# Output projection: which engine makes four combinations of y, and where its weight slots lie

## The chip, the core and the metric

One core of a Trainium2 chip runs the whole kernel. The core has a matrix engine (TensorE; PE in the profile, its weight loads PEld), a vector engine (VectorE, DVE), an activation engine (ScalarE, ACT), a general engine (GpSimd, POOL) and a queue that issues the transfers (SyncE, SP). Each engine takes its own instructions strictly in the order in which they stand in its queue, and waits on semaphores for the others. The metric is the device time of one execution in microseconds.

## What is computed

The reference is one layer of a hybrid decoder for 512 tokens (T) of width 2048 (D): a windowed attention branch and a gated DeltaNet branch, merged by gates, and one last projection that is added to the residual stream:

```python
y_a = a_out @ w_o_swa
y_b = o.reshape(B, T, DN_VAL).astype(x.dtype) @ w_o_dn
y = jax.nn.sigmoid(mg_a) * y_a + jax.nn.sigmoid(mg_b) * y_b
return x + gate * (y @ w_out)
```

The change concerns the last two lines. All matrix products are made to nearly full float32 accuracy: each operand is split into a high part (a rounding cast, on ScalarE) and a low part (operand minus high part, on VectorE), and three matmuls, high by high, high by low and low by high, add up in PSUM. This split is the helper at L52 and L53, and the three matmuls are L223 to L225; so work of many places in the program shows under these lines.

## The kernel before

The kernel runs through a start, the DeltaNet, its output projection, the attention, and the method `finish`, in which the change lies. `finish` has two stages.

**The stage ahead** makes y. It goes through 16 tiles j of 128 channels by 512 tokens. For each, `channel_tile` multiplies the attention's output, which lies in the tiles hh and hl (16 x 512 elements per partition each), by 2048 rows of a weight (raw, loaded from in_w_os, 1 MB). The product (PSUM tile mm) gets gated and merged with the other branch (m and yb, each loaded from DRAM; L1226 and L1227), and y's tile is stored to DRAM (y_d, L1228). Its first 256 tokens are split at once into a11 (j below 8) or a12 (j from 8 on), and for j below 8 the sum of its two token halves is split into s3.

**The output stage** multiplies y by w_out (2048 x 2048) by a scheme of seven products in place of eight, for two halves n of the columns. With y cut into four blocks (channels below and above 1024, tokens below and above 256; `lo` and `hi` are the token halves), the left operands are a11, a12, a22, and four combinations s1 = a21 - a22, s2 = -(s1) - a11, s3 = a11 + a21, s4 = a21 - a22 + a11 - a12. The right operands are sums of quarters of w_out that lie in slots a, b and c of two 1 MB tiles each (raw for slot a, rawb and rawc for the others):

```python
order = [
    ("m1", "a11", "a", []),
    ("m7", "s3", "b", [add("a", "b"), add("b", "c")]),
    ("m5", "s1", "a", []),
    ("m2", "a12", "b", []),
    ("m6", "s2", "a", [add("a", "c")]),
    ("m4", "a22", "b", [add("b", "a")]),
    ("m3", "s4", "c", []),
]
```

Each product has four pieces p. A piece needs its sums (VectorE, L1286, 128 x 1024 each), its split into whi (ScalarE, L52) and wlo (VectorE, L53), and then takes 12 matmuls of 128 x 512. There are three pairs of whi and wlo, so a split can start when the piece three before it is done. With 7 products of 4 pieces and two halves, that is 56 pieces and 672 matmuls. When a product is done, `evict` combines it with others (VectorE), multiplies by the gate (L1336), adds the residual x on GpSimd (L1339) and stores to out.

The four combinations that the output stage needs late are made inside it, by the generator `combos`, one step of which is taken per piece. It goes twice over eight tiles kt. Each time it loads y[kt] (ya, L1248) and y[kt+8] (yc, L1250) again from DRAM, 256 KB each; the first pass makes s1 and s2, the second a22 and s4. All the arithmetic is VectorE's, on 128 x 256: four instructions per kt in the first pass and five in the second (L1252 to L1258 and the low parts L53), with two casts on ScalarE. The results go into the room of hh and hl, which the projections no longer read by then: in the profile they are `hh` and `hl` in this stage too.

Slots b and c have a pool of their own (fraw), and slot a is the pair of raw buffers of the projections. The program is written with a layer that puts each engine's instructions in order by itself, so the order on an engine is not that of the code.

Of the kernel before, what the change touches and what calls it, by code (L numbers as in the profile page):

```python
# [16 lines left out]
P = 128  # L17
T = 512
# [18 lines left out]
class Layer:  # L37
# [222 lines left out]
    def build(self):  # L260
        tc, nc, a = self.tc, self.nc, self.a
        with ExitStack() as es:
            self.const = es.enter_context(tc.tile_pool(name="const", bufs=1))
            self.dram = es.enter_context(tc.tile_pool(name="scratch", bufs=1, space=DRAM))
            self.dnc_es = ExitStack()
            self.dnc = self.dnc_es.enter_context(tc.tile_pool(name="dnc", bufs=1, side="right"))
            self.v_d = self.dram.tile([2, P, T], F32, name="v_d")
            self.hpool = es.enter_context(tc.tile_pool(name="h", bufs=1))
            hh = self.hh = self.hpool.tile([P, KT, T], F32R, name="hh")
            hl = self.hl = self.hpool.tile([P, KT, T], F32R, name="hl")  # L270
# [24 lines left out]
            self.attention()  # L295
            if self.stop == "attention":
                return
            self.finish()
# [911 lines left out]
    def finish(self):  # L1210
        tc, nc, a = self.tc, self.nc, self.a
        with ExitStack() as es:
            yp = es.enter_context(tc.tile_pool(name="fy", bufs=1, reuse_waits="tile"))
            wk = es.enter_context(tc.tile_pool(name="fwk", bufs=2, reuse_waits="tile"))
            quad = lambda pool, name: tuple(pool.tile([P, 8, 256], F32R, name=name + x) for x in "hl")
            A = {n: quad(yp, n) for n in ("a11", "s3", "a12")}
            lo, hi = slice(0, 256), slice(256, 512)
            with ExitStack() as eo:
                self.pmm = eo.enter_context(tc.tile_pool(name="pmmf", bufs=2, space=PSUM, reuse_waits="tile"))
                for j in range(KT):  # L1220
                    m = wk.tile([P, T], F32, tag="m", name="m")
                    nc.sync.dma_start(out=m, in_=self.ma_d[j])
                    yb = wk.tile([P, T], F32, tag="yb", name="yb")
                    nc.sync.dma_start(out=yb, in_=self.yb_d[j])
                    ps = self.channel_tile(f"os{j}")
                    nc.vector.scalar_tensor_tensor(out=m, in0=m, scalar=1.0, in1=ps, op0=ALU.add, op1=ALU.mult)  # L1226
                    nc.vector.tensor_tensor(out=m, in0=m, in1=yb, op=ALU.add)  # L1227
                    nc.sync.dma_start(out=self.y_d[j], in_=m)  # L1228
                    h, l = A["a11" if j < 8 else "a12"]
                    self.split(h[:, j % 8, :], l[:, j % 8, :], m[:, lo])  # L1230
                    if j < 8:
                        h, l = A["s3"]
                        nc.vector.tensor_tensor(out=yb[:, lo], in0=m[:, lo], in1=m[:, hi], op=ALU.add)
                        self.split(h[:, j, :], l[:, j, :], yb[:, lo])
            v = lambda i: (self.hh[:, 4 * i : 4 * i + 4, :], self.hl[:, 4 * i : 4 * i + 4, :])
            for i, n in enumerate(("s1", "s2", "s4", "a22")):
                A[n] = tuple(x.rearrange("p a (b t) -> p (a b) t", b=2) for x in v(i))
            self.output(es, wk, A)

    def combos(self, wk, A):  # L1240

        nc = self.nc
        lo, hi = slice(0, 256), slice(256, 512)
        TT = nc.vector.tensor_tensor
        for second in range(2):
            for kt in range(8):
                p = wk.tile([P, T], F32, tag="m", name="ya")
                nc.sync.dma_start(out=p, in_=self.y_d[kt])  # L1248
                q = wk.tile([P, T], F32, tag="yb", name="yc")
                nc.sync.dma_start(out=q, in_=self.y_d[kt + 8])  # L1250
                yield
                TT(out=p[:, hi], in0=p[:, hi], in1=q[:, hi], op=ALU.subtract)  # L1252
                if second:
                    TT(out=p[:, lo], in0=p[:, hi], in1=p[:, lo], op=ALU.add)
                    TT(out=p[:, lo], in0=p[:, lo], in1=q[:, lo], op=ALU.subtract)
                    self.split(A["a22"][0][:, kt, :], A["a22"][1][:, kt, :], q[:, hi])
                else:
                    nc.vector.scalar_tensor_tensor(  # L1258
                        out=p[:, lo], in0=p[:, hi], scalar=-1.0, in1=p[:, lo], op0=ALU.mult, op1=ALU.subtract
                    )  # L1260
                    self.split(A["s1"][0][:, kt, :], A["s1"][1][:, kt, :], p[:, hi])
                n = "s4" if second else "s2"
                self.split(A[n][0][:, kt, :], A[n][1][:, kt, :], p[:, lo])

    def output(self, es, wk, A):
# [3 lines left out]
        fr = es.enter_context(tc.tile_pool(name="fraw", bufs=1, reuse_waits="tile"))  # L1269
        slots = {}  # L1270

        def load(slot, c, r, nchunk):

            for i in range(2):
# [56 lines left out]
        gt = wk.tile([P, 2, T], F32, tag="gt", name="gt", bufs=1)  # L1331

        def columns(n, c, t, src, sign):

# [7 lines left out]
        def evict(n, name):  # L1342
            TT = nc.vector.tensor_tensor
            for t in range(2):
# [2 lines left out]
                    o = t * 1024 + n * T  # L1347
                    nc.sync.dma_start(out=gt[:, t, :], in_=self.gate_d[o : o + T].partition_broadcast(P))
                if name in ("m1", "m5"):
                    k = wk.tile([P, T], F32, tag=f"{name}{t}", name=name, bufs=1)  # L1350
# [156 lines left out]
```

## Time and profile before

| | us |
|---|---|
| median of 3 runs | 2985.4 (2984.39 to 2986.28) |
| the profiled execution, its own time | 2983.21 |
| its span, from the first to the last instruction | 2980.8 |
| PE busy in the span | 2876.5 (97%) |
| DVE busy | 1788.7 (60%) |
| ACT busy | 1084.7 (36%) |
| POOL busy | 245.3 (8%) |
| output stage, from the first matmul of m1 to the span's end | 2806.9 to 2980.8 |

A row of the timeline gives start, duration, engine, line, operation and tiles, and in brackets how long the engine had been idle and what released it. A row of windows gives a stretch, its length, then for each engine the busy time with the number of instructions, the granted clock of PE, the share of the DMA engines and GB/s. A DVE instruction's row begins some 0.08 us before the one in front of it ends, so its step is a little shorter than its duration. An engine that is blocked inside an instruction counts as busy.

### The profile page before, as it was taken

The numbers are of one execution on the slowest core, as the hardware profiler recorded it, in microseconds if no ns is written. First come the engines' busy times: TensorE is split into PE (matmuls) and PEld (weight loads), VectorE is DVE, ScalarE is ACT, GpSimd is POOL, SyncE is SP. The second block draws the span as 40 slices with busy tenths as digits, with TensorE's granted clock in tenths as the row PEclk, the third lists the DMA queues.
The fourth block names the chain that finished last, engine by engine and source line by source line (L and its number), as shares of the span: only waits on it lengthen the run. The fifth ranks groups of instructions, "written<-read, shape, count | busy, mean of one in ns | idle before, by whom it ended". The sixth has DMA issues, their size and how long they took to land.

```text
span 2980.8 us, 37958 instructions
## 1 busy us (share of the span) xinstructions
PE 2876.5 (97%) x14524; PEld 2355.1 (79%) x14524; DVE 1788.7 (60%) x2903; ACT 1084.7 (36%) x2101; POOL 245.3 (8%) x204
## 2 busy tenths in 40 slices
PE   6899889999999999999999999999999999999988
PEld 5687777777788888888888878888787788788877
DVE  5855898899554444445554453433756656554697
ACT  3354333233433333333333322311334444432343
POOL 0012121201000000001100000000100000000013
PEclk8999999999999999999999999999999999999999
DMA  9855545733533333334332476554322223375562
GB/s 330 315 166 179 172 139 159 204 100 114 152 123 122 107 121 107 125 114 135 114 123 101 166 274 208 185 172 163 110 87 87 85 91 101 113 256 172 177 200 96
DMA packets 176231, 452.17 MB, mean 152 GB/s; under 512 B 74257, under 2 KB 76817, under 8 KB 140209
## 3 DMA queue, kind: packets, MB, share of 16 engines
q1 hardware_dynamic: 176050, 449.76, 45.9%
q8 instruction: 114, 1.87, 0.3%
q14 instruction: 67, 0.55, 0.1%
HBM read 388.00 MB, written 59.46 MB: 150 GB/s over the span
## 4 chain that ended last, share of the span: by engine, by line
PE 79%; DVE 11%; DMA 4%; issue 2%; ACT 2%; POOL 1%; SPq 1%; POOLq 0%; DVEq 0%; ACTq 0%
PE mm L223 22%; PE mm L225 22%; PE mm L224 22%; DVE wlo L53 3%; DVE atmp L705 2%; DVE A L711 1%; DVE wa L387 1%; PE S L1147 1%; DMA E<-g_rows 1%; PE O L1198 1%; PE pv L858 1%; PE po L877 1%; ACT whi L52 1%; PE pP L257 1%; DMA silu_d<-silu_c 1%
## 5 line engine op out<-in xcount | busy, mean ns | idle before, releaser
L223 PE MATMUL mm<-hh,whi 128*128 128x512 f32 x2784 | 1134.8, 408 | 0.7 <-ACT mth L246 0.7
L225 PE MATMUL mm<-hh,wlo 128*128 128x512 f32 x2784 | 1093.5, 393 | 0.0
L224 PE MATMUL mm<-hl,whi 128*128 128x512 f32 x2784 | 1092.0, 392 | 0.0
L53 DVE TENSOR_TENSOR wlo<-raw,whi 128x1024 fp32r<-128x1024 f32 (+1 forms) x452 | 551.2, 1222 | 500.3 <-ACT whi L52 484.4
L52 ACT CAST whi<-raw 128x1024 fp32r<-128x1024 f32 (+1 forms) x452 | 470.5, 1043 | 958.8 <-PE mm L224 906.6
L225 PEld LDWEIGHTS mm<-hh,wlo 128*128 128x128 f32 x2784 | 525.1, 189 | 113.9 <-issue 0.4
L223 PEld LDWEIGHTS mm<-hh,whi 128*128 128x128 f32 x2784 | 526.4, 189 | 110.8 <-issue 8.4
L224 PEld LDWEIGHTS mm<-hl,whi 128*128 128x128 f32 x2784 | 527.0, 189 | 99.7 <-issue 0.6
L223 PE MATMUL mm<-oh,whi 128*128 128x512 f32 x512 | 200.4, 393 | 2.7 <-ACT oh L52 1.8
L225 PE MATMUL mm<-oh,wlo 128*128 128x512 f32 x512 | 199.2, 389 | 0.5 <-DVE wlo L53 0.5
L224 PE MATMUL mm<-ol,whi 128*128 128x512 f32 x512 | 199.1, 389 | 0.0
L805 POOL TENSOR_TENSOR qe<-qe,yq 128x512 f32<-128x512 f32 x32 | 49.9, 1577 | 929.3 <-DMA qe<-eg_rows 867.8
L674 POOL TENSOR_TENSOR E<-E,neg_g 128x512 f32<-128x512 f32 x64 | 76.9, 1202 | 489.5 <-DMA E<-g_rows 446.1
L223 PEld LDWEIGHTS mm<-oh,whi 128*128 128x128 f32 x512 | 96.1, 188 | 24.5 <-ACT oh L52 2.6
L225 PEld LDWEIGHTS mm<-oh,wlo 128*128 128x128 f32 x512 | 96.1, 188 | 21.3 <-DVE wlo L53 1.0
L224 PEld LDWEIGHTS mm<-ol,whi 128*128 128x128 f32 x512 | 96.1, 188 | 20.7 <-issue 1.0
L705 DVE TENSOR_TENSOR atmp<-A 128x62 f32<-128x62 f32 (+30 forms) x124 | 110.4, 890 | 2.0
L711 DVE TENSOR_TENSOR A<-A,atmp 128x62 f32<-128x62 f32 (+30 forms) x124 | 109.9, 886 | 1.8
L851 DVE SCALAR_TENSOR_TENSOR r<-pp,neg_eg,vt 128x128 f32<-128x128 f32 x96 | 29.3, 346 | 81.2 <-PE pp L848 79.4
L550 DVE SCALAR_TENSOR_TENSOR yv<-mm,convh,yv 128x511 f32<-128x511 f32 (+2 forms) x96 | 71.4, 744 | 8.1 <-ACT yv L547 6.6
L1171 ACT ACTIVATE sm<-sm,mx,rs 128x256 f32<-128x256 f32 (+1 forms) x128 | 71.7, 562 | 3.3 <-DVE mx L1166 3.3
L1414 DVE SCALAR_TENSOR_TENSOR gate_bc<-gw,silu_c,gate_bc 128x2048 f32<-128x2048 f32 x15 | 35.3, 2351 | 40.9 <-DMA gw<-in_w_ada_gate 40.9
(328 smaller groups left out, 3167.2 us busy)
## 6 DMA issues: line engine op xcount, KB each, us to landing
raw<-in_w_ch SPq DMA_DIRECT2D x158, 1024.0 KB
wa<-in_w_ada_ss SPq DMA_DIRECT2D x32, 1024.0 KB
raw<-in_w_od SPq DMA_DIRECT2D x32, 1024.0 KB
E<-g_rows SPq DMA_DIRECT2D x64, 256.0 KB
gw<-in_w_ada_gate SPq DMA_DIRECT2D x16, 1024.0 KB
raw<-in_w_os SPq DMA_DIRECT2D x16, 1024.0 KB
qe<-eg_rows SPq DMA_DIRECT2D x32, 256.0 KB
o_d<-zh SPq DMA_DIRECT2D x32, 256.0 KB
```

The costliest lines, as they stand in the source:

```text
L52: self.nc.scalar.copy(out=hi, in_=src)
L53: self.nc.vector.tensor_tensor(out=lo, in0=src, in1=hi.bitcast(F32), op=ALU.subtract)
L223: nc.tensor.matmul(ps, lhsT=wh, rhs=xh, start=first, stop=False)
L224: nc.tensor.matmul(ps, lhsT=wh, rhs=xl, start=False, stop=False)
L225: nc.tensor.matmul(ps, lhsT=wl, rhs=xh, start=False, stop=last)
L550: nc.vector.scalar_tensor_tensor(out=y[:, s:], in0=ps[:, : T - s], scalar=w[:, j : j + 1], in1=y[:, s:], op0=ALU.mult, op1=ALU.add)
L674: nc.gpsimd.tensor_tensor(out=E, in0=E, in1=ng, op=ALU.add)
L705: eng.tensor_tensor(out=t, in0=A[:, m : m + 1, m + 1 :].to_broadcast([P, m, n]), in1=A[:, :m, m : m + 1].to_broadcast([P, m, n]), op=ALU.mult,
L711: eng.tensor_tensor(out=A[:, :m, m + 1 :], in0=A[:, :m, m + 1 :], in1=t, op=ALU.add)
L805: nc.gpsimd.tensor_tensor(out=qf, in0=qf, in1=q, op=ALU.mult)
L1171: nc.scalar.activation(t, t, AF.Exp, scale=r[:, h : h + 1], bias=mx[:, h : h + 1], accum_out=den[:, h : h + 1])
L1414: nc.vector.scalar_tensor_tensor(out=acc, in0=w, scalar=s, in1=acc, op0=ALU.mult, op1=ALU.add)
```

## The change

Four things are changed.

1. s1 and s2 are made in the stage ahead, in its last eight tiles. For j from 8 on, y[j-8] is loaded again (yq, 256 KB, one buffer), and behind the split of a12 VectorE does two combinations and two low parts of 128 x 256 and ScalarE two casts. They get tiles of their own.
2. a22 and s4 are still made in the output stage, in one pass over eight kt, by GpSimd and ScalarE: per kt GpSimd does one 128 x 512 subtraction, one 128 x 256 sum and two low parts of 128 x 256, ScalarE two casts.
3. The room of hh and hl is given free behind the last tile of the stage ahead (the pool h now lies above the weight pools and is closed there), and a new pool fx in that room takes a22, s4, slots b and c, the gate gt and the kept copies of m1 and m5. The pools fy and fwk go to the other side of the memory.
4. The first two weight tiles of slot a are jobs of the projections' weight queue, so the first four pieces are loaded and split as those of the stage ahead are.

```diff
         jobs += [(f"os{j}", a["w_os"][j]) for j in range(KT)]
+        jobs += [(f"out{i}", a["w_out"][0, i]) for i in range(2)]
...
+            self.h_es = es.enter_context(ExitStack())
+            self.hpool = self.h_es.enter_context(tc.tile_pool(name="h", bufs=1))
+            self.hh = self.hpool.tile([P, KT, T], F32R, name="hh")
+            self.hl = self.hpool.tile([P, KT, T], F32R, name="hl")
...
+                    if j >= 8:
+                        q = wk.tile([P, T], F32, tag="yq", name="yq", bufs=1)
+                        nc.sync.dma_start(out=q, in_=self.y_d[j - 8])
...
+                    else:
+                        nc.vector.tensor_tensor(out=q[:, hi], in0=q[:, hi], in1=m[:, hi], op=ALU.subtract)
+                        put("s1", q[:, hi])
+                        nc.vector.scalar_tensor_tensor(
+                            out=q[:, lo], in0=q[:, hi], scalar=-1.0, in1=q[:, lo], op0=ALU.mult, op1=ALU.subtract
+                        )
+                        put("s2", q[:, lo])
+            self.h_es.close()
+            fx = es.enter_context(tc.tile_pool(name="fx", bufs=1, reuse_waits="tile"))
+            for n in ("a22", "s4"):
+                A[n] = quad(fx, n)
+            self.output(es, wk, fx, A)
...
+        TT = nc.gpsimd.tensor_tensor
+
+        def put(n, kt, src):
+            h, l = A[n][0][:, kt, :], A[n][1][:, kt, :]
+            nc.scalar.copy(out=h, in_=src)
+            TT(out=l, in0=src, in1=h.bitcast(F32), op=ALU.subtract)
+
+        for kt in range(8):
+            p = wk.tile([P, T], F32, tag="m", name="ya")
+            nc.sync.dma_start(out=p, in_=self.y_d[kt])
+            q = wk.tile([P, T], F32, tag="yb", name="yc")
+            nc.sync.dma_start(out=q, in_=self.y_d[kt + 8])
+            yield
+            put("a22", kt, q[:, hi])
+            TT(out=p, in0=p, in1=q, op=ALU.subtract)
+            yield
+            TT(out=p[:, lo], in0=p[:, lo], in1=p[:, hi], op=ALU.add)
+            put("s4", kt, p[:, lo])
...
+            if i < 4:
+                ready[i] = self.half(f"out{i // 2}")
+                self.half_used += 1
+                return
...
-        next(side, None)
-        load("a", 0, 0, 0)
-        load("b", 1, 0, 0)
-        load("c", 1, 1, 0)
+        for i in range(2):
+            slots["a", i] = self.raws[len(self.jobs) - 2 + i]
+            load("b", 1, 0, 0, (i,))
+            load("c", 1, 1, 0, (i,))
+        self.due = []
```

The order of the instructions moves at three places. The rows below give line, operation, tiles and shape; lines are those of each program itself (L1288 of the changed program is L1279 before, the loads into the slots; L1228 and L1233 store y; L1224 and L1226 of the changed program load m and yb).

The transfer queue (SP) around the end of the stage ahead, before:

```order
L1279 DMA raw<-in_w_out 128x2048
L1228 DMA y_d<-m 128x512
L1250 DMA yc<-y_d 128x512
L1248 DMA ya<-y_d 128x512
L1250 DMA yc<-y_d 128x512
L1248 DMA ya<-y_d 128x512
L1228 DMA y_d<-m 128x512
```

and now:

```order
L184 DMA raw<-in_w_out 128x2048
L1233 DMA y_d<-m 128x512
L1267 DMA yc<-y_d 128x512
L1265 DMA ya<-y_d 128x512
L1229 DMA yq<-y_d 128x512
L1288 DMA rawb<-in_w_out 128x2048
L1233 DMA y_d<-m 128x512
L1288 DMA rawc<-in_w_out 128x2048
L1288 DMA rawb<-in_w_out 128x2048
L1288 DMA rawc<-in_w_out 128x2048
L1265 DMA ya<-y_d 128x512
L1267 DMA yc<-y_d 128x512
```

The four loads of slots b and c stood some 60 transfers earlier, among the first tiles of the stage ahead. Now the first of them comes behind the last yq and three stand behind the store of the last y tile; the loads of the second kt (ya, yc) stand behind all four.

The casts of ScalarE from m2's first piece to its last, before (hh are the high parts of the combinations, COPY keeps m5):

```order
L52 CAST whi<-rawb 128x1024
L52 CAST hh<-ya 128x256
L52 CAST hh<-yc 128x256
L52 CAST whi<-rawb 128x1024
L52 CAST hh<-ya 128x256
L1351 COPY m_22311<-m_22189 128x512
L52 CAST whi<-rawb 128x1024
L1351 COPY m_22313<-m_22190 128x512
L52 CAST hh<-yc 128x256
L52 CAST whi<-rawb 128x1024
```

and now (m2's last three pieces):

```order
L1260 CAST a22h<-yc 128x256
L52 CAST whi<-rawb 128x1024
L1260 CAST s4h<-ya 128x256
L1260 CAST a22h<-yc 128x256
L1365 COPY m_22313<-m_22215 128x512
L1260 CAST s4h<-ya 128x256
L52 CAST whi<-rawb 128x1024
L1365 COPY m_22315<-m_22216 128x512
L1260 CAST a22h<-yc 128x256
L1260 CAST s4h<-ya 128x256
L52 CAST whi<-rawb 128x1024
```

All sixteen casts of the combinations now stand ahead of the cast of m2's last piece; before, the last of them stood behind the casts of m4's second piece. An s4h now waits for GpSimd where the casts of before waited for VectorE.

GpSimd, which had nothing between the attention and the first residual sum (L1339, after m2), before:

```order
L1339 TENSOR_TENSOR c_22424<-c_22424,x 128x512
L1339 TENSOR_TENSOR c_22431<-c_22431,x 128x512
L1339 TENSOR_TENSOR c_22511<-c_22511,x 128x512
L1339 TENSOR_TENSOR m_22084<-m_22084,x 128x512
L1339 TENSOR_TENSOR c_22522<-c_22522,x 128x512
```

has 32 instructions ahead of these now, four for each kt, of which these are the second and third kt:

```order
L1270 TENSOR_TENSOR ya<-ya,yc 128x512
L1261 TENSOR_TENSOR a22l<-yc,a22h 128x256
L1272 TENSOR_TENSOR ya<-ya 128x256
L1261 TENSOR_TENSOR s4l<-ya,s4h 128x256
L1270 TENSOR_TENSOR ya<-ya,yc 128x512
L1272 TENSOR_TENSOR ya<-ya 128x256
L1261 TENSOR_TENSOR a22l<-yc,a22h 128x256
L1261 TENSOR_TENSOR s4l<-ya,s4h 128x256
```

On VectorE the combinations' instructions are gone from the output stage (4 x 8 and 5 x 8 of 128 x 256), and four per tile stand behind the low part of a12 in the last eight tiles of the stage ahead.

More of the change, by code (lines that the diff above doesn't have):

```diff
@@ L1212, in finish @@
         with ExitStack() as es:
-            yp = es.enter_context(tc.tile_pool(name="fy", bufs=1, reuse_waits="tile"))
-            wk = es.enter_context(tc.tile_pool(name="fwk", bufs=2, reuse_waits="tile"))
+            yp = es.enter_context(tc.tile_pool(name="fy", bufs=1, side="right", reuse_waits="tile"))
+            wk = es.enter_context(tc.tile_pool(name="fwk", bufs=2, side="right", reuse_waits="tile"))
             quad = lambda pool, name: tuple(pool.tile([P, 8, 256], F32R, name=name + x) for x in "hl")
-            A = {n: quad(yp, n) for n in ("a11", "s3", "a12")}
+            A = {n: quad(yp, n) for n in ("a11", "s3", "a12", "s1", "s2")}
             lo, hi = slice(0, 256), slice(256, 512)
@@ L1228, in finish @@
                     nc.sync.dma_start(out=self.y_d[j], in_=m)
-                    h, l = A["a11" if j < 8 else "a12"]
-                    self.split(h[:, j % 8, :], l[:, j % 8, :], m[:, lo])
+                    put = lambda n, src: self.split(A[n][0][:, j % 8, :], A[n][1][:, j % 8, :], src)
+                    put("a11" if j < 8 else "a12", m[:, lo])
                     if j < 8:
-                        h, l = A["s3"]
                         nc.vector.tensor_tensor(out=yb[:, lo], in0=m[:, lo], in1=m[:, hi], op=ALU.add)
[L1234 to L1238, printed above, removed]
+                        put("s3", yb[:, lo])
+                    else:
[10 more added lines that the diff above has]
+            self.output(es, wk, fx, A)
     def combos(self, wk, A):
@@ L1243, in combos @@
         lo, hi = slice(0, 256), slice(256, 512)
[L1244 to L1263, printed above, removed]
@@ L1265, in output @@
-    def output(self, es, wk, A):
+        TT = nc.gpsimd.tensor_tensor
[14 more added lines that the diff above has]
+            put("s4", kt, p[:, lo])
@@ L1267, in output, with load @@
+    def output(self, es, wk, fr, A):
         tc, nc, a = self.tc, self.nc, self.a
         pf = es.enter_context(tc.tile_pool(name="pfo", bufs=1, space=PSUM, reuse_waits="tile"))
-        fr = es.enter_context(tc.tile_pool(name="fraw", bufs=1, reuse_waits="tile"))
         slots = {}
-        def load(slot, c, r, nchunk):
-            for i in range(2):
+        def load(slot, c, r, nchunk, parts=(0, 1)):
+            for i in parts:
                 if slot == "a":
@@ L1330, in output @@
         ps = {}
-        gt = wk.tile([P, 2, T], F32, tag="gt", name="gt", bufs=1)
+        gt = fr.tile([P, 2, T], F32, name="gt")
         def columns(n, c, t, src, sign):
@@ L1349, in evict @@
                 if name in ("m1", "m5"):
-                    k = wk.tile([P, T], F32, tag=f"{name}{t}", name=name, bufs=1)
+                    k = fr.tile([P, T], F32, tag=f"{name}{t}", name=name, bufs=1)
                     nc.scalar.copy(out=k, in_=b)
```

3 lines of the change are left out of this document (removed).

## The prediction

> **What bounds the kernel now.** I went from the profile's page (PE 97% busy) to the windows of the last stages:
>
> ```profile
> core 0: us, PE busy (x) PEld busy (x) DVE busy (x) ACT busy (x) POOL busy (x), PEclk, DMA share, GB/s
> 2750.00:2780.00 30.00, 30.00 (x134) 24.84 (x133) 11.01 (x14) 6.74 (x9) 0.00 (x0) 1.00 0.56 182
> ...
> 2840.00:2860.00 20.00, 19.77 (x87) 15.82 (x86) 20.00 (x39) 11.93 (x20) 0.00 (x0) 1.00 0.51 143
> 2860.00:2880.00 20.00, 14.56 (x57) 11.61 (x56) 19.94 (x27) 6.89 (x10) 3.10 (x2) 0.83 0.75 225
> 2880.00:2900.00 20.00, 18.19 (x80) 14.74 (x80) 19.75 (x23) 6.71 (x7) 6.13 (x4) 1.00 0.76 287
> ...
> 2940.00:2960.00 20.00, 20.00 (x90) 16.57 (x89) 17.22 (x20) 7.59 (x8) 5.66 (x3) 1.00 0.28 79
> ```
>
> The stage ahead (first row) is PE's, with VectorE busy 37%. In the first half of the output stage VectorE is full (20.00 of 20) and PE has holes; in the second PE is full again. How much is lost comes from the matmuls by tiles, whole stage first and then from 2891 on, and from ScalarE's timeline where PE sets the pace:
>
> ```profile
> L223 PE MATMUL m<-whi,a11h x32: 389/389/389, 2806.9 to 2905.0; 128*128 128x512 f32 x32
> L223 PE MATMUL m<-whi,hh x128: 387/389/632, 2828.7 to 2972.5; 128*128 128x512 f32 x128
> ...
> L223 PE MATMUL m<-whi,a11h x16: 389/389/389, 2894.8 to 2905.0; 128*128 128x512 f32 x16
> ...
> 2940.76 1.05 ACT L52 CAST whi<-raw 128x1024 fp32r<-128x1024 f32 x1 [1.67 <-PE m L225]
> 2943.48 1.06 ACT L52 CAST whi<-raw 128x1024 fp32r<-128x1024 f32 x1 [1.67 <-PE m L225]
> ```
>
> A piece takes PE 2.72 us (2943.48 - 2940.76), a half of 28 pieces 76.2. The first half runs from 2806.9 (its m1) to 2894.8 (the next m1): 87.9, so 11.7 of waiting. The second runs to the last L223 at 2972.5 and two matmuls more: 2.4 of waiting. The whole change can win at most these 14 us, 0.5%, and the question is who feeds the pieces of the first half in time.
>
> **What it takes off VectorE.** Durations of the first half (groups by line), and steps from the timeline:
>
> ```profile
> L53 DVE TENSOR_TENSOR wlo<-raw,whi 128x1024 fp32r<-128x1024 f32 x11 | 13.5, 1223 | 0.0
> L53 DVE TENSOR_TENSOR hl<-ya,hh 128x256 fp32r<-128x256 f32 x23 | 9.6, 424 | 0.0
> L52 ACT CAST hh<-ya 128x256 fp32r<-128x256 f32 x22 | 8.8, 405 | 10.7 <-DVE ya L1252 5.3 <-DVE ya L1255 3.0 <-DVE ya L1258 2.3
> ...
> 2850.61 0.42 DVE L53 TENSOR_TENSOR hl<-yc,hh 128x256 fp32r<-128x256 f32 x1
> 2850.95 0.43 DVE L1254 TENSOR_TENSOR ya<-ya 128x256 f32<-128x256 f32 x1
> ...
> 2902.00 1.22 DVE L1286 TENSOR_TENSOR raw<-raw,rawb 128x1024 f32<-128x1024 f32 x1
> 2903.14 1.22 DVE L53 TENSOR_TENSOR wlo<-rawb,whi 128x1024 fp32r<-128x1024 f32 x1
> ```
>
> Back to back, 256 elements cost VectorE 0.34 us (2850.95 - 2850.61) and 1024 cost 1.14 (2903.14 - 2902.00). Of the 72 combination instructions three are done before 2806.9, so 69 x 0.34 = 23.5 us leave a stretch in which VectorE was full. That is the gain on offer.
>
> s1 and s2 go to the stage ahead: 4 x 0.34 = 1.4 us of VectorE and 0.8 of ScalarE in each of eight tiles that last four pieces' time, 10.9 us, with VectorE at 37%. The load of yq stands ahead of the next weight load and waits until the tile before has made its s2:
>
> ```profile
> 2730.94 0.69 DVE L1226 SCALAR_TENSOR_TENSOR m<-m,mm 128x512 f32<-128x512 f32 x1 [3.31 <-PE mm L225]
> ...
> 2738.55 0.33 SPq L183 DMA_DIRECT2D raw<-in_w_os  x1
> ```
>
> The weight load goes 7.6 us behind the end of the tile's matmuls; s2 is done about 4.5 behind it (L1226, L1227 and wlo 2.5, then a12 and four short ones with two casts between). The eight loads of 256 KB are 24 GB/s over these 87 us, beside 182 at a DMA share of 0.56, and as many leave the output stage. I cost all this at nothing. Without that cover it would be 8 x 1.4 = 11 us.
>
> **What it puts on GpSimd.** No 128 x 256 sum of GpSimd is in the trace; these rows bound it, and show how it runs beside VectorE:
>
> ```profile
> 178.83 1.05 POOL L674 TENSOR_TENSOR E<-E,neg_g 128x512 f32<-128x512 f32 x1 [178.39 <-DMA E<-g_rows]
> ...
> L602 POOL MEMSET tt<- 64x256 f32 x4 | 1.1, 306 | 14.1 <-PE ptk L257 14.1
> L1019 POOL MEMSET partner<- 128x512 f32 x2 | 1.0, 536 | 463.3 <-PE mm L225 463.3
> ...
> 2870.00 1.21 DVE L53 TENSOR_TENSOR wlo<-rawb,whi 128x1024 fp32r<-128x1024 f32 x1
> 2871.14 2.29 DVE L1286 TENSOR_TENSOR rawb<-rawb,raw 128x1024 f32<-128x1024 f32 x1
> ...
> 2870.51 1.84 POOL L1339 TENSOR_TENSOR c<-c,x 128x512 f32<-128x512 f32 x1 [2.11 <-DMA out<-c]
> ...
> 2866.23 0.69 DVE L1336 SCALAR_TENSOR_TENSOR c<-c,gt 128x512 f32<-128x512 f32 x1
> 2866.83 0.68 DVE L1355 TENSOR_TENSOR c<-m,m 128x512 f32<-128x512 f32 x1
> ...
> 2867.13 1.26 POOL L1339 TENSOR_TENSOR c<-c,x 128x512 f32<-128x512 f32 x1 [380.85 <-DVE c L1336]
> ```
>
> The two engines take turns. GpSimd starts at 2870.51, VectorE's split ends at 2871.21, GpSimd ends at 2872.35, 1.14 later, and VectorE's sum, begun at 2871.14, takes 2.29 in place of 1.22. So a sum of 512 takes 1.14 us in which neither the splits nor the sums of VectorE move. For 256 I take 0.6 (the fills at 256 and 512 stand at 0.57; half of 1.14), between 0.53 (half of the 1.05 at 178.83, with VectorE idle) and 1.14 (if the width costs nothing). A kt is then 1.14 + 3 x 0.6 = 2.94 us of such time. Each of its four instructions also waits for the one ahead of it or a cast: 0.22 from the end of L1336 (2866.92) to GpSimd's start (2867.13), and for the VectorE instruction that runs: VectorE has some 19 us of work in the 35 us that follow, so 55% of the time it is inside a 1.14 us instruction, half of which is left: 0.3. Together 2.94 + 4 x 0.5 = 5.0 us per kt, more than PE's 2.72 per piece.
>
> [...]
>
> **The start of the stage.** Slots b and c may now be filled only when the last tile's matmuls have read hh and hl, at 2807.3. Before, they were loaded here:
>
> ```profile
> 2637.78 0.43 SPq L1279 DMA_DIRECT2D rawb<-in_w_out  x1
> ...
> 2656.60 0.42 SPq L1279 DMA_DIRECT2D rawc<-in_w_out  x1
> ...
> 2964.62 3.07 DMA x<-in_x
> ...
> GB/s 330 315 166 179 172 139 159 204 100 114 152 123 122 107 121 107 125 114 135 114 123 101 166 274 208 185 172 163 110 87 87 85 91 101 113 256 172 177 200 96
> ```
>
> 256 KB alone land in 3.07 us (chain of waits); at the 330 GB/s of the first slice another 0.79 MB take 2.4, so the first 1 MB lands at 2807.4 + 5.5 = 2812.9 and the next ones 3.2 apart: c0 2816.1, b1 2819.3, c1 2822.5, and yc and ya of the second kt, queued behind them, 2824.1. m7's first piece needs c0, two sums, and wlo: 2816.1 + 3 x 1.14 = 2819.5, against 2818.3, when PE has done the two matmuls that need whi alone: 1.2 late. The third needs c1, and its cast stands behind a22h of the second kt (2824.1 + 0.4 + 1.05, then wlo 1.14 = 2826.7, wanted at 2825.0): 1.7 late. The fourth's cast stands behind s4h of that kt, three GpSimd instructions on: 2824.1 + 3.9 + 0.4 + 1.05 = 2829.5, its wlo 2830.6, wanted at 2829.2: 1.4 late. **Sum 4.3 us** by the time m5 begins; 1.2 if the loads land sooner, 6 if later.
>
> **The chain through GpSimd.** The weight loads for m2 wait in SP for m7's last split (2830.6), and the third kt's ya and yc wait behind them: the second of these 1 MB loads and two of 256 KB land at about 2838. From there GpSimd alone sets the pace: kt 3 to 6 in 4 x 5.0, and three of kt 7's four instructions, 3.9: 2861.9. Then s4h (0.4) and the cast of m2's last piece behind it (1.05): 2863.4. Without any wait PE would start that piece at 2806.9 + 15 x 2.72 = 2847.7. So it starts **15.7 us late**, the 4.3 included. From there VectorE has 14 wlo, about 2 sums and 18 instructions of 512 in the evictions (at 0.6, 2866.83 - 2866.23) and GpSimd 5 x 1.14 of the residual: 16 + 2.3 + 10.8 + 5.7 = 34.8 us for the 13 pieces' 35.4: full, and I add 2 for unevenness. First half: 17.7 of waiting against 11.7; second half as before. **+6.0 us.** The profiled 2983.21 becomes 2989.2; the median of before lies 2.2 above that run, so the time is 2985.4 + 6.0 = 2991.4, and I say 2991.5.
>
> The bounds: with 0.53, 1.05 and no waiting for VectorE a kt is 1.05 + 1.6 + 0.9 = 3.5; the last piece of m2 starts some 8 us late and the half loses 9: 2.7 less than before, 2983. With 1.14 for each it is 6.6, and the half loses 26: +14, 2999.
>
> **The rivals.** *GpSimd finds its time for nothing (faster).* If its instructions fit between VectorE's and the casts are not late, the 23.5 us off VectorE count: about 5 us of waiting are left in the first half, -6.7, 2978.7. For it: VectorE falls to 55%. Against: four dependent instructions per kt would have to fit in 2.72 us, and 2.94 is their bare time.
>
> *GpSimd is starved (slower still).* This row is one 512 sum that VectorE did not let in:
>
> ```profile
> 2901.19 11.13 POOL L1339 TENSOR_TENSOR m<-m,x 128x512 f32<-128x512 f32 x1 [3.75 <-DMA x<-in_x]
> ...
> 2911.21 2.19 DVE L53 TENSOR_TENSOR wlo<-rawb,whi 128x1024 fp32r<-128x1024 f32 x1
> ```
>
> VectorE ran ready instructions without a gap until 2911.2. One such row in the chain from kt 3 on adds 10 us, since it has no slack: 3001. It decides as soon as VectorE runs ahead of PE there; against it stands that its splits wait for a cast in every piece.
>
> **How the numbers follow.** A measurement of this kernel can tell 0.2% (6.0 us) from no change. The chain as reckoned, between its bounds, has 0.60, a little more than half of it above +6.0: 0.34 slower, 0.26 same. The free fit has 0.27, of it 0.18 faster than 0.2% and 0.09 same. Starvation has 0.13, slower. So faster 0.18, same 0.35, slower 0.47. The range, from just above the free fit to past one starved row, is 2980 to 3004; the likeliest case's own is 2983 to 2999.
>
> **What would show it.** m7's first rawc issued behind the last y store at about 2809; casts of m2's last two pieces released by GpSimd; a row of GpSimd's 256 near 0.6 undisturbed; second half's m1 starting near 2901; no new wait of PE before 2806. It is wrong if VectorE is again 20.00 of 20 in the first half with PE's holes behind it, if a kt takes GpSimd under 3.5 us, or if the casts come in time.

## The result and the profile after

The changed kernel takes 2993.2 us (median of 9 runs, 2988.59 to 2998.07), the kernel before beside it 2984.4 (9 runs, 2981.16 to 2988.48). The ratio, estimated over all runs, is 1.0026, 95% interval 1.0017 to 1.0034 (the two medians alone give 1.0029): slower, the likeliest of the forecast's three outcomes; 2991.5 us was forecast.

| | before | after |
|---|---|---|
| the profiled execution, its span (us) | 2980.8 | 2986.8 |
| first matmul of m1 to the span's end | 173.9 | 185.9 |
| waiting in the first half, beyond 28 x 2.72 | 11.8 | 21.0 |
| the same in the second half | 2.4 | 5.1 |
| POOL busy | 245.3 | 281.4 |

The output stage grew by 12.0 us. The profiled executions differ by only 6.0, because this one of the changed kernel, the fastest of its nine, began the stage 6.0 us sooner (2800.9 against 2806.9). That is no effect of the change: in the eleven profiles of this study the stage begins between 2800.9 and 2811.0, and three of kernels with the same program up to there (before, and two variants of it that only shift addresses) begin it at 2806.9, 2811.0 and 2805.2, while the change and four variants of it that are the same up to there but for the first of the eight kt (kernels 1 to 4 below) begin it between 2800.9 and 2807.9.

The windows of the changed kernel, one row for the stage ahead, then m1 to m5, m2, and m6 to the end of the first half:

```profile
core 0: us, PE busy (x) PEld busy (x) DVE busy (x) ACT busy (x) POOL busy (x), PEclk, DMA share, GB/s
2700.00:2800.00 100.00, 100.00 (x443) 82.78 (x442) 49.50 (x77) 29.11 (x43) 2.86 (x2) 1.00 0.57 184
...
2804.60:2841.00 36.40, 31.68 (x127) 24.27 (x126) 35.55 (x28) 14.22 (x21) 21.62 (x14) 0.95 0.65 237
2841.00:2865.10 24.10, 16.49 (x53) 11.70 (x52) 13.13 (x9) 8.23 (x14) 17.83 (x16) 0.79 0.23 76
2865.10:2898.10 33.00, 33.00 (x146) 27.01 (x144) 30.63 (x31) 12.64 (x12) 11.11 (x6) 1.00 0.75 241
```

The stage ahead stays without a hole of PE. VectorE is almost full up to 2841, half idle while PE waits in m2, and PE has no hole after that. The starts of the products' first matmuls (groups by tiles; the last row is the first product of the second half alone) say how much each takes:

```profile
L224 PE MATMUL m<-whi,a11h x32: 394/394/395, 2800.9 to 2908.6; 128*128 128x512 f32 x32
L224 PE MATMUL m<-whi,s3h x32: 388/394/629, 2813.1 to 2923.1; 128*128 128x512 f32 x32
L224 PE MATMUL m<-whi,s1h x32: 394/396/400, 2830.4 to 2934.3; 128*128 128x512 f32 x32
L224 PE MATMUL m<-whi,a12h x32: 389/394/796, 2841.6 to 2945.5; 128*128 128x512 f32 x32
L224 PE MATMUL m<-whi,s2h x32: 394/397/400, 2865.1 to 2956.7; 128*128 128x512 f32 x32
...
L224 PE MATMUL m<-whi,a11h x16: 394/394/395, 2898.1 to 2908.6; 128*128 128x512 f32 x16
```

Four pieces need 10.9. m7 took 17.3 (2830.4 - 2813.1) and m2 23.5 (2865.1 - 2841.6): these two hold 19 of the 21 us. m5 took 11.2 though nothing of it waits, of which more below. PE's holes in m2 (us in total, how many, the longest) are these:

```profile
PE m L224 <- ACT whi L52: 5.1, 2, 3.7
PE m L225 <- DVE wlo L53: 2.5, 3, 1.4
```

A wlo is made from the whi, so both go back to the cast; of the rest of m2's 12.6 us some 3 are matmuls that come slower behind the holes (last section, 15 matmuls at 0.20). What the casts waited for stands in ScalarE's timeline:

```profile
2844.30 0.41 ACT L1260 CAST s4h<-ya 128x256 fp32r<-128x256 f32 x1 [6.31 <-POOL ya L1272]
...
2844.91 1.04 ACT L52 CAST whi<-rawb 128x1024 fp32r<-128x1024 f32 x1
...
2853.94 0.40 ACT L1260 CAST s4h<-ya 128x256 fp32r<-128x256 f32 x1 [2.64 <-POOL ya L1272]
2854.25 1.04 ACT L52 CAST whi<-rawb 128x1024 fp32r<-128x1024 f32 x1
...
2859.75 0.40 ACT L1260 CAST s4h<-ya 128x256 fp32r<-128x256 f32 x1 [3.67 <-POOL ya L1272]
2860.06 1.04 ACT L52 CAST whi<-rawb 128x1024 fp32r<-128x1024 f32 x1
```

Each of m2's later casts (whi) stands behind an s4h cast that GpSimd releases, directly or with one short cast between (a22h in the first of the three). And GpSimd is late because it runs like this beside VectorE (GpSimd's timeline, its fourth kt and then a stretch in which VectorE waits itself; behind it VectorE's timeline at the fourth kt):

```profile
2832.41 2.19 POOL L1270 TENSOR_TENSOR ya<-ya,yc 128x512 f32<-128x512 f32 x1 [2.44 <-DMA yc<-y_d]
2834.68 1.61 POOL L1272 TENSOR_TENSOR ya<-ya 128x256 f32<-128x256 f32 x1
2836.25 1.72 POOL L1261 TENSOR_TENSOR a22l<-yc,a22h 128x256 fp32r<-128x256 f32 x1
2837.93 1.72 POOL L1261 TENSOR_TENSOR s4l<-ya,s4h 128x256 fp32r<-128x256 f32 x1
...
2851.28 1.26 POOL L1270 TENSOR_TENSOR ya<-ya,yc 128x512 f32<-128x512 f32 x1
2852.50 0.72 POOL L1261 TENSOR_TENSOR a22l<-yc,a22h 128x256 fp32r<-128x256 f32 x1
```

```profile
2832.23 1.22 DVE L53 TENSOR_TENSOR wlo<-raw,whi 128x1024 fp32r<-128x1024 f32 x1
...
2837.40 1.65 DVE L1295 TENSOR_TENSOR raw<-raw,rawc 128x1024 f32<-128x1024 f32 x1
2838.97 1.76 DVE L53 TENSOR_TENSOR wlo<-rawb,whi 128x1024 fp32r<-128x1024 f32 x1
```

A 256-wide sum takes GpSimd 0.72 alone and 1.72 beside a working VectorE, a 512-wide one 1.26 and 2.19: each waits about one microsecond more, almost the whole step (1.13 to 1.15) of one 1024-wide VectorE instruction. VectorE's instruction behind it takes 1.76 in place of 1.22. So in this stretch the engines alternate, one instruction each. They don't always: the sum that VectorE kept out for 11.13 us in the kernel before is found again in kernels 4, 6 and 8 below (11.0 to 11.2 us, the same sum of the residual, at the second half's start, each time while VectorE runs ready instructions without a gap). What decides between the two wasn't tried.

### The profile page after: what moved, and what is told of

Its sections match the earlier page's. It is cut to its first block, busy times and chain, and to the rows that moved or that the text cites. A ratio compares the mean times of both kernels' runs of the same rounds, so it can differ in the third digit from the quotient of the medians.

```text
span 2986.8 us, 37938 instructions
## 1 busy us (share of the span) xinstructions
PE 2881.2 (96%) x14524; PEld 2355.9 (79%) x14524; DVE 1790.3 (60%) x2863; ACT 1084.3 (36%) x2101; POOL 281.4 (9%) x236
## 4 chain that ended last, share of the span: by engine, by line
PE 77%; DVE 9%; DMA 6%; POOL 3%; ACT 2%; issue 2%; SPq 1%; POOLq 0%; DVEq 0%; ACTq 0%
PE mm L224 22%; PE mm L226 21%; PE mm L225 21%; DVE wlo L53 2%; DMA E<-g_rows 2%; DVE atmp L707 1%; DVE A L713 1%; DVE wa L389 1%; PE S L1149 1%; ACT whi L52 1%; PE O L1200 1%; PE pv L860 1%; PE po L879 1%; PE pP L258 1%; DMA silu_d<-silu_c 1%
## 5 line engine op out<-in xcount | busy, mean ns | idle before, releaser
L389 DVE SCALAR_TENSOR_TENSOR wa<-wa,silu_cb 128x2048 f32<-128x2048 f32 x24 | 54.8, 2282 | 7.0 <-DMA silu_cb<-silu_d 7.0
```

Source lines behind the costliest of these rows:

```text
L389: nc.vector.scalar_tensor_tensor(out=wa, in0=wa, scalar=1.0, in1=scb, op0=ALU.mult, op1=ALU.mult, accum_out=t[:, j : j + 1])
```

## Experiments

Lines of the changed kernel are used. "Waits" of a product are the time from the start of its first matmul to that of the next product's, less 4 x 2.72 us, and for the second half up to the end of its last matmul, less 28 x 2.72. All columns are in us. Numbers of kernels are those of this table. The second pass is the one that makes a22 and s4.

| | m1 | m7 | m5 | m2 | m6 | m4 | m3 | second half | stage, us |
|---|---|---|---|---|---|---|---|---|---|
| before | 0.0 | 0.0 | 1.4 | 0.1 | 0.7 | 7.5 | 2.1 | 2.4 | 173.9 |
| the change | 1.3 | 6.5 | 0.3 | 12.6 | 0.3 | 0.1 | 0.0 | 5.1 | 185.9 |
| 1: second pass on VectorE | 0.3 | 3.6 | 0.3 | 0.3 | 0.3 | 0.0 | 3.1 | 6.2 | 173.9 |
| 2: low parts on VectorE | 0.3 | 8.7 | 0.3 | 3.8 | 0.3 | 0.0 | 1.4 | 6.1 | 180.7 |
| 3: VectorE rounds m2, m6 | 1.3 | 6.4 | 0.3 | 8.9 | 1.8 | 0.0 | 0.0 | 6.1 | 184.7 |
| 4: GpSimd casts a22h, s4h | 1.3 | 4.8 | 0.3 | 1.8 | 15.4 | 0.0 | 0.0 | 1.8 | 185.2 |
| 5: the change, 32 bytes on | 1.3 | 6.1 | 0.3 | 12.7 | 0.3 | 0.0 | 0.0 | 4.4 | 184.8 |
| 6: before, 32 bytes on | 0.3 | 0.3 | 2.7 | 0.3 | 0.6 | 8.8 | 1.5 | 2.8 | 177.0 |
| 7: as 1, 160 bytes on | 0.2 | 3.6 | 0.0 | 0.0 | 0.0 | 0.0 | 3.9 | 5.0 | 172.4 |
| 8: before, all 32 bytes on | 0.0 | 0.0 | 2.2 | 0.0 | 0.9 | 8.9 | 1.2 | 2.4 | 175.3 |
| 9: as 1, 416 bytes, b early | 0.0 | 1.2 | 0.0 | 0.0 | 0.0 | 0.0 | 1.6 | 5.0 | 167.5 |

**1. The second pass on VectorE.**

```diff
-        TT = nc.gpsimd.tensor_tensor
+        TT = nc.vector.tensor_tensor
```

> The change with the whole second pass (the sums of a22 and s4 and their low parts) on VectorE, nothing of it on GpSimd. Chain theory: the 12.6 us that TensorE waits in m2 come from ScalarE's casts of m2's pieces standing behind s4h casts that wait for GpSimd, whose every sum first waits for a whole 1024-wide VectorE instruction (1.72 us for a 256-wide one instead of 0.72). Then m2's waits fall under 2 us, m7's 6.4 us stay, VectorE takes 40 x 0.34 = 13.6 us more of its own and loses none to GpSimd; the first half waits about 8 us instead of 21.0 and the time is about 2981 us, 0.999 of before. Rival, VectorE is the bound again: m2's waits go, but 5 to 10 us come back in m5, m6 and m4 as in the kernel before (11.8 us there), and the time is 2986 to 2991. Rival, the y loads are what is late (yc of kt 3 was waited for): m2 still waits 6 us or more.

2982.9 us, ratio 0.9992 (0.9982 to 1.0002). m2's 12.6 us are gone (0.3), m7 waits 3.6 in place of 6.5, and nothing comes back in m5, m6 or m4: the first half waits 8.0, as expected. The y loads are not what was late. VectorE, which got 32 instructions of 256 or 512 elements more, does not miss the time, since it no longer waits for GpSimd. Its groups in the first half, first of the change, then of this kernel:

```profile
L53 DVE TENSOR_TENSOR wlo<-rawb,whi 128x1024 fp32r<-128x1024 f32 x12 | 19.2, 1604 | 12.1 <-ACT whi L52 12.0
...
L1295 DVE TENSOR_TENSOR raw<-raw,rawc 128x1024 f32<-128x1024 f32 x4 | 6.7, 1682 | 0.1
```

```profile
L53 DVE TENSOR_TENSOR wlo<-rawb,whi 128x1024 fp32r<-128x1024 f32 x12 | 15.6, 1310 | 0.1
...
L1295 DVE TENSOR_TENSOR raw<-raw,rawc 128x1024 f32<-128x1024 f32 x4 | 4.9, 1221 | 0.0
```

The same 16 instructions take 25.9 us in the change and 20.5 here, and in the change VectorE idles 12 us behind ScalarE's casts. A low part costs VectorE 0.34 us when it makes it itself, and 0.54 (1.76 - 1.22) when GpSimd makes it beside it.

**2. Only the low parts on VectorE**, the two sums of a kt still on GpSimd.

```diff
             nc.scalar.copy(out=h, in_=src)
-            TT(out=l, in0=src, in1=h.bitcast(F32), op=ALU.subtract)
+            nc.vector.tensor_tensor(out=l, in0=src, in1=h.bitcast(F32), op=ALU.subtract)
```

> The change with the low parts of a22 and s4 on VectorE and only the two sums of each kt on GpSimd. Chain theory: GpSimd's work for a kt falls from 7.2 to about 2.2 + 1.7 = 3.9 us, under the two pieces (5.5 us) that it has; the s4h casts come in time, m2 waits under 3 us, VectorE has 16 x 0.34 = 5.4 us more; the first half waits about 8 us and the time is about 2981 us, 0.999 of before. Rival, the sums alone already hold ScalarE up, since each waits for its turn with VectorE: m2 still waits 5 us or more, time 2985 to 2990. Rival, VectorE is the bound: waits of 5 us or more in m6 and m4.

2990.5 us, ratio 1.0017 (1.0009 to 1.0026); expected 2981. m2's wait falls to 3.8, near the 3 of the chain theory, but m7's rises to 8.7. VectorE's timeline there shows the two sums of m7's last pieces and the low part behind them:

```profile
2823.66 3.98 DVE L1295 TENSOR_TENSOR rawb<-rawb,rawc 128x1024 f32<-128x1024 f32 x2
2827.57 1.49 DVE L1261 TENSOR_TENSOR a22l<-yc,a22h 128x256 fp32r<-128x256 f32 x1
```

Two instructions that take 2.35 undisturbed took 3.98 between GpSimd's turns, and the low part, 0.42 undisturbed, took 1.49 ahead of the next wlo, in the stretch in which the late slots leave VectorE no slack. The theory had counted the turns in m2 alone.

**3 and 4: is it ScalarE's order, or GpSimd's turns at VectorE?** Experiment 1 removed both. Two kernels leave GpSimd its work and take m2's casts out of its way. In 3, VectorE rounds the high parts of m2's and m6's weights in the first half:

```diff
-            self.split(hi, lo, piece(slot, p))
+            if n == 0 and name in ("m2", "m6"):
+                nc.vector.tensor_copy(out=hi, in_=piece(slot, p))
+                nc.vector.tensor_tensor(out=lo, in0=piece(slot, p), in1=hi.bitcast(F32), op=ALU.subtract)
+            else:
+                self.split(hi, lo, piece(slot, p))
```

> The change with GpSimd's second pass as it is, but in the first half the high parts of the weights of m2 and m6 rounded by VectorE instead of ScalarE, so that these eight casts no longer stand behind s4h casts on ScalarE. Chain theory (ScalarE's order carries GpSimd's lateness to TensorE): m2's 12.6 us of waiting fall under 2 us although GpSimd does the same work as late as before (each kt still 6 to 7 us, last sum near 60 us after the stage's first matmul); nothing comes in their place as long as the last s4 part is done before m3 needs it; the first half waits 8 to 11 us, time 0.999 to 1.000 of before. [...] Rival, the wait only moves: m2 is rid of it, but m4 waits 6 us or more for a22, or m2's eviction for a buffer.

2995.2 us, ratio 1.0033 (1.0021 to 1.0046). m2 still waits 8.9, where the chain theory has under 2, and no longer for ScalarE: VectorE is now full. The window from 2846 on, with columns as above:

```profile
2846.00:2866.00 20.00, 14.27 (x52) 10.03 (x51) 19.93 (x13) 3.20 (x8) 18.81 (x13) 0.93 0.29 80
```

The experiment was not clean: VectorE's rounding takes 1.13 for a piece too, so a piece of m2 cost it three such steps, 3.4 us against 2.72, before any turn of GpSimd's. In 4, GpSimd casts a22h and s4h itself, and nothing on ScalarE waits for it:

```diff
-            nc.scalar.copy(out=h, in_=src)
+            nc.gpsimd.tensor_copy(out=h, in_=src)
```

> The change with the 16 casts of a22h and s4h on GpSimd instead of ScalarE, so that nothing on ScalarE waits for GpSimd, while GpSimd has two more instructions for each kt (9 to 11 us for a kt in place of 6 to 7). Chain theory: ScalarE's casts of m2's pieces come in time and m2's waits of 12.6 us fall to under 4 us (what is left is VectorE, whose two 1024-wide instructions for a piece, each with a turn of GpSimd behind it, take 2 x (1.13 + 0.55) = 3.4 us against 2.72). GpSimd then ends 20 us or more later, and m6 or m4 wait for it (m2's eviction for a buffer of ya, m4 for a22), so that the time need not fall: 2990 to 3005. Rival, GpSimd's turns at VectorE are what holds m2 up: m2 still waits 8 us or more.

2996.7 us, ratio 1.0042 (1.0027 to 1.0056). m2's wait falls from 12.6 to 1.8 although GpSimd works in it as before and still takes its turns, as in this low part of a piece of m2 (1.22 undisturbed):

```profile
2844.56 1.75 DVE L53 TENSOR_TENSOR wlo<-rawb,whi 128x1024 fp32r<-128x1024 f32 x1
```

That settles it for m2: ScalarE's order carried GpSimd's lateness to PE. GpSimd now ends later, and the wait moves to the place that the expectation named. VectorE's longest wait in the first half, in total, how often, and the longest single one:

```profile
DVE c L1369 <- POOL s4l L1261: 13.0, 2, 9.3
```

m2's eviction (L1369) needs a buffer that GpSimd still reads as ya; m6's splits stand behind it on VectorE, and m6 waits 15.4. GpSimd's length is then paid in another engine's queue.

**5 to 8: what makes the pieces longer that wait for nothing?** From the change's m1 on, pieces of m1, m7, m5, m2 and m6 take 2.80 us, those of m4 and m3 2.72. Steps of ScalarE's casts, which PE releases there:

```profile
2870.88 1.05 ACT L52 CAST whi<-rawb 128x1024 fp32r<-128x1024 f32 x1 [1.75 <-PE m L226]
2873.68 1.05 ACT L52 CAST whi<-rawb 128x1024 fp32r<-128x1024 f32 x1 [1.75 <-PE m L226]
...
2887.41 1.06 ACT L52 CAST whi<-rawc 128x1024 fp32r<-128x1024 f32 x1 [1.66 <-PE m L226]
2890.13 1.06 ACT L52 CAST whi<-rawc 128x1024 fp32r<-128x1024 f32 x1 [1.66 <-PE m L226]
```

The left operands of the first five lie in the pool on the right side, and the allocation puts a11h at byte 147424 of a partition, 224 beyond a multiple of 256; the weight tiles (34368), a22 and s4 (58944 on) lie 64 beyond one. Before, all of them did. In 5 a pad of 32 bytes shifts the right pools (a11h at 147392, 192 beyond); in 6 a pad of 32 bytes shifts only a11, s3 and a12 of the kernel before (a11h at 124512, 96 beyond):

```diff
+            pad = es.enter_context(tc.tile_pool(name="pad", bufs=1, side="right"))
+            pad.tile([P, 8], F32, name="pad")
             yp = es.enter_context(tc.tile_pool(name="fy", bufs=1, side="right", reuse_waits="tile"))
```

> The change with 32 bytes of padding on the right side of SBUF, so that the ten tiles of a11, s3, a12, s1 and s2 begin at multiples of 64 bytes (147392 in place of 147424 for a11's high part). Nothing else moves in time. Alignment theory: the 0.08 us that each piece of m1, m7, m5, m2 and m6 takes beyond 2.72 us comes from left operands that begin 32 bytes off a multiple of 64; it goes, in both halves, 40 x 0.08 = 3.2 us in all, time about 2990 us, 1.0015 of before. Place theory: the right end of SBUF, or its distance from the weight tiles, is what costs; the pieces keep 2.80 us and the time is that of the change, 1.0026 of before.

> The kernel before with 32 bytes of padding ahead of its projections' pool on the left side, so that a11, s3 and a12 begin 32 bytes off a multiple of 64 (124512 in place of 124480); s1, s2, a22 and s4 stay where they are. Alignment theory: pieces of m1, m7 and m2 take 2.80 in place of 2.72 us where they don't wait for something else, those of m5, m6, m4 and m3 stay; up to 24 x 0.08 = 1.9 us, less what hides in the waits of the first half, time 1.0003 to 1.0006 of before. Place theory: no piece changes, time 1.0000 of before.

5 took 2994.2 us, 1.0029 (1.0017 to 1.0041): the pieces still take 2.79, so being at a multiple of 64 isn't enough. 6 took 2985.8, 1.0003 (0.9995 to 1.0012), too little to tell by the time, but its matmuls do: m1, m7 and m2 now take 2.80 for a piece, and m5, m6, m4 and m3, which weren't shifted, none of it. Matmuls of m1 in the second half, before and then in 6:

```profile
2897.78 0.39 PE L224 MATMUL m<-wlo,a11h 128*128 128x512 f32 x1
2898.01 0.39 PE L225 MATMUL m<-whi,a11l 128*128 128x512 f32 x1
2898.24 0.39 PE L223 MATMUL m<-whi,a11h 128*128 128x512 f32 x1
2898.46 0.39 PE L224 MATMUL m<-wlo,a11h 128*128 128x512 f32 x1
```

```profile
2903.68 0.40 PE L223 MATMUL m<-whi,a11h 128*128 128x512 f32 x1
2903.92 0.40 PE L224 MATMUL m<-wlo,a11h 128*128 128x512 f32 x1
2904.15 0.40 PE L225 MATMUL m<-whi,a11l 128*128 128x512 f32 x1
2904.38 0.40 PE L223 MATMUL m<-whi,a11h 128*128 128x512 f32 x1
```

Three steps are 0.68 before and 0.70 here. 7 is kernel 1 with a pad of 160 bytes (a11h at 147264, 64 beyond a multiple of 256, like the weights):

> The change with the second pass on VectorE (as in the run before of that kind) and 160 bytes of padding on the right side of SBUF: a11's high part begins at byte 147264 of a partition, which is 64 beyond a multiple of 256, as the weight tiles (34368) and a22 and s4 (58944 on) are; with 32 bytes of padding it was 192 beyond one. Theory of the place within 256 bytes: pieces of m1, m7, m5, m2 and m6 that wait for nothing take 2.72 in place of 2.80 us, about 3 us less in all, time 0.998 of before. Rival, a coarser place or the right side itself: they keep 2.78 to 2.80 us and the time is 0.999 of before.

Every piece that waits for nothing is back at 2.72, and kernel 7's distance is an odd multiple of 256, while the 128 of kernel 5 still cost 0.07 a piece: so it is the place within 256 bytes, not within 128 or 512. The time is 2982.8 us, 0.9993 (0.9984 to 1.0002), against 0.9992 of kernel 1. The stage is 1.5 us shorter, not 3: in the first half VectorE is the limit at its end, and m3 waits 0.8 more. That is less than a median can show. 8 puts the pad of 32 bytes ahead of the projections' input in the kernel before, so that both operands of each product move together:

> The kernel before with 32 bytes of padding ahead of the projections' input, so that the input (18016), the weight tiles (99936 on), the output projection's inputs and the left operands all begin 96 beyond a multiple of 256 instead of 64: each pair of operands of a three-fold product keeps its distance. Theory of the distance (what costs is that the two operands of a matmul begin at different places within 256 bytes): nothing changes, pieces of 2.72 us, matmuls 227 ns apart, time 1.000 of before. Theory of the place itself (an operand that doesn't begin at a multiple of 64 costs): about 9,600 matmuls of the projections and 672 of the output stage are 5 to 6 ns further apart, 50 to 60 us in all, time 1.017 to 1.020 of before.

2983.7 us, 0.9999 (0.9990 to 1.0009), pieces of 2.72 us: the place itself (96 in place of 64 bytes beyond a multiple of 256) cost nothing, the distance between the two operands within 256 bytes did (0.07 to 0.08 us a piece). Only the time per piece shows this; the times of the whole kernels don't tell 5 from the change, 6 from before or 7 from 1.

**9. Part of slot b loaded early.** Kernel 1 with a pad of 416 bytes, and the first half of slot b in 8 KB of its own:

```diff
+            fb = es.enter_context(tc.tile_pool(name="fb", bufs=1, side="right", reuse_waits="tile"))
...
+                    if j == 10:
+                        b0 = fb.tile([P, 2048], F32, tag="b0", name="rawb")
+                        nc.sync.dma_start(out=b0, in_=a["w_out"][2, 0])
                     ps = self.channel_tile(f"os{j}")
...
-            load("b", 1, 0, 0, (i,))
             load("c", 1, 1, 0, (i,))
+            if i == 0:
+                slots["b", 0] = b0
+                load("b", 1, 0, 0, (1,))
```

> As the run beside it (second pass on VectorE), with 416 bytes of padding (a11's high part at 147008, 64 beyond a multiple of 512) and the first half of slot b in 8 KB of its own on the right, loaded in the stage ahead (at tile 10 of the projection), so that three loads of 1 MB in place of four stand behind the last matmul of the projection. If the place within 512 bytes matters, the pieces take 2.72 us here even if the run beside it keeps 2.80. Start theory: m7's pieces wait for the slots' loads and the sums behind them; the waits of 0.9, 0.5 and 2.1 us in m7 of the first half come to under 1.5 us in all, 2 to 3 us less than in the run beside it. Rival, VectorE's own backlog (eight sums of 1.13 us and the eight low parts within four pieces) is what m7 waits for: its waits stay at 3 us or more.

2973.9 us, ratio 0.9972 (0.9962 to 0.9983): faster than both kernels. m7 waits 1.2 in place of 3.6, as the start theory has it, m3 1.6 in place of 3.9, and the stage is 4.9 us shorter than in 7. The gain in m3 wasn't forecast and its cause wasn't tried; nor is the rest of the 8.9 us between the medians of 7 and 9, which lies ahead of the stage. PE's waits for VectorE in its stage, written as above, come to 5.1; for other engines there are 0.2:

```profile
PE m L225 <- DVE wlo L53: 5.1, 5, 1.5
```

## Why the prediction came out

**The first half loses, through the chain it named.** m2's last casts were to stand behind s4h casts that GpSimd releases, and do. The last piece of m2 was to start 15.7 us late; it started at 2861.7 (PE's timeline below), which is 2800.9 + 15 x 2.72 and 20.0 us. Step by step from the stage's first matmul: the loads that the chain starts from came as forecast (the fourth kt, kt 3 in the prediction, could begin after 31.5 us; forecast 2838 - 2806.9 = 31.1); from there to the last s4h took 27.3 us (2832.41 to 2859.75) where 23.9 were forecast; and from that s4h to the piece 2.0 where 1.5 were, with PE still in the slow matmuls of the piece before. The first half was to wait 17.7 and waited 21.0; the second half's m1 came at 2898.1, or 97.2 us after the first's, where 94 was forecast. For two things in these 21.0 us the prediction had no term: the address effect (1.6 in each half) and the slow matmuls of the last section (4.2).

**The mis-sized term is GpSimd's wait for its turn.** A kt was taken as 2.94 us of bare work and 4 x 0.5 of waiting, 0.3 of it for VectorE (half an instruction, 55% of the time): 5.0, with 6.6 as the upper bound. A 256-wide sum undisturbed was forecast at 0.6 and is 0.72, and a 512-wide one at 1.14 and is 1.26; but the wait for VectorE is 1.0 for nearly every instruction, since VectorE was not 55% busy there: 35.55 of 36.40 us up to 2841, much of it because GpSimd's turns stretch it. The fourth kt ran from 2832.41 to 2839.65, 7.2 us, beyond the bound. Only when VectorE itself ran out of work (m2) did a kt fall to 3.8 to 5.9 us, which made up for some of the error. One of the prediction's signs of being wrong came true in part, a full VectorE with PE's holes (m7's) behind it; the other two, a kt under 3.5 us and casts in time, did not.

**The start** was to cost 4.3 us by m5, bounds 1.2 to 6, and cost 7.8 (m1 and m7), of which 0.6 is the address effect. The transfers were issued where forecast, behind the stage's first matmul and the last y store (the last two loads follow within 1.0 us of these rows):

```profile
2800.87 0.33 SPq L1288 DMA_DIRECT2D rawb<-in_w_out  x1
2802.55 0.32 SPq L1233 DMA_DIRECT2D y_d<-m  x1
2802.92 0.42 SPq L1288 DMA_DIRECT2D rawc<-in_w_out  x1
```

In kernel 1, with the same loads, m1 and m7 wait 3.9; so about half of the 7.8 come with GpSimd's pass. Its turns stretch VectorE's weight sums there, for which the prediction had no term; in the change one at 2816.46 takes 2.32 us and two at 2818.70 take 3.42, against 1.22 and 2.35 undisturbed. Some 1.2 us of that half (an estimate, six matmuls at 0.20) are the slow matmuls behind m7's holes, of which the last section tells. Of the other half, 2.4 go in m7 when one of the four loads comes earlier (kernel 9 against 7).

**At nothing: confirmed.** s1 and s2 and their loads cost the stage ahead nothing (PE 100.00 of 100, above).

**After m2** it put 2 us of unevenness; there are 0.4, all of it the address effect. **The second half "as before"** was wrong by 2.8 us: 1.6 of address effect (20 pieces x 0.08), and m7 waits 3.3 beyond it where it waited 2.2. What makes up that last 1.1 wasn't tried.

**The rivals.** GpSimd did not find its time for nothing: without its help, with the pass on VectorE, the time is 2982.9, and with it 2993.2. None of its 32 sums was starved: the longest took 2.27 us, held up by one VectorE instruction.

That 2991.5 lies so near 2993.2 is partly luck: the stage grew by 12.0 in the profiles where 6.0 was reckoned, and the medians differ by 8.8; the differing starts (2800.9 to 2811.0) hide part of the 12.0.

## What to carry to other kernels

Before moving sums to GpSimd, price them in turns: beside a VectorE that streams 1024-wide instructions, a 256-wide sum cost 1.7 us here and took 0.54 from VectorE, more than the 0.34 for which VectorE does it. Never let a cast that feeds PE stand in an in-order queue behind one that waits for such a sum (m2 waited 12.6 us so, and 1.8 without, in kernel 4). After a move to another pool, look whether matmuls that wait for nothing still come at the same step, and compare the addresses of both operands within 256 bytes (2.80 us a piece here in place of 2.72).

## What the runs showed of the hardware

In these kernels a matmul of 128 x 512 came every 0.227 us where its two operands begin at the same place within 256 bytes, and about every 0.233 where not: 0.07 to 0.08 us for a piece of 12, at 32, 128 and 160 bytes of distance (kernels 6, 5 and the change), nothing at 0 (kernels 7, 8 and 9). Other distances weren't tried.

Some holes cost PE more than their length. The end of m2 in the changed kernel's PE timeline:

```profile
2855.34 0.80 PE L224 MATMUL m<-whi,a12h 128*128 128x512 f32 x1 [3.68 <-ACT whi L52]
2857.51 0.79 PE L225 MATMUL m<-wlo,a12h 128*128 128x512 f32 x1 [1.37 <-DVE wlo L53]
2858.10 0.63 PE L226 MATMUL m<-whi,a12l 128*128 128x512 f32 x1
2858.53 0.63 PE L224 MATMUL m<-whi,a12h 128*128 128x512 f32 x1
...
2861.48 0.40 PE L226 MATMUL m<-whi,a12l 128*128 128x512 f32 x1
2861.72 0.39 PE L224 MATMUL m<-whi,a12h 128*128 128x512 f32 x1
```

Behind the hole the matmuls come every 0.43 us for some 3 us, then every 0.24 again; the granted clock, averaged over m2, is 0.79. There are three such stretches in the changed kernel's first half (before, one), with 21 matmuls of 0.62 us or more in all, at 0.20 us each 4.2 of its 21.0 us. This one stands behind holes of 3.68 and 1.37 us; the other two stand behind shorter ones, of 1.90 and 1.49 us in m7 and of 1.44 and 0.82 earlier in m2, each with one or two matmuls between. Holes of 1.56 and 1.48 in m7 of kernel 4, and single ones of 1.69 in kernel 1 and 1.81 in the kernel before, had no slow matmuls behind them, so which holes bring them stays open. A forecast of waiting has to add a price for this: 1.2 to 1.6 us for a stretch here (an estimate, 6 to 8 matmuls at 0.20).
